# Adds joined in pairs, two down tiles interleaved, six raw weight slots, and another planner for the queues

## The chip, the core and the metric

The kernel runs on one core of a Trainium2 chip. A core has a matrix engine (TensorE, PE, with a queue of its own for loading weights, PEld), a vector engine (VectorE, DVE), a scalar engine (ScalarE, ACT), GpSimd (POOL) and SyncE (SP), which here issues the DMAs. Each works through a queue of its own, and semaphores make one wait for another. TensorE accumulates into banks of PSUM; the other operands lie in SBUF. The metric is the time of one execution on the device, in microseconds. The time before is 2044.98 us, the median of 3 runs (2036.12 to 2045.60).

## What is computed

One layer of a decoder trunk on 2048 tokens of 1024 channels, with 16 learned tokens put ahead and dropped at the end, all in float32:

```
u = rmsnorm(h);  p = u @ w_in                       # 1024 -> 1792
y_a = pool mixer (windows 2, 4, 8, 16)               of p_pool
y_b = conv of 31 taps, layer norm, silu, matrix      of p_bval * sigmoid(p_bgate)
y_c = gelu(p_cgate) * linear scan (conv of 4 taps, two gates)   of p_cx
h = h + concat(y_a, y_b, y_c) @ w_out                # 1024 -> 1024
h = h + square(relu(rmsnorm(h) @ w_up)) @ w_down     # 1024 -> 4096 -> 1024
out = rmsnorm(h)[16:]
```

## The kernel before

**Arithmetic.** A float32 operand is split into a high part (ACT, L108) and a low part (DVE, L109), and a product is three matmuls: high·high, high·low, low·high. A block of weights comes by DMA into a raw slot (tile `wr`, `WR` = 4 of them), and its two parts go into a split slot (tile `wh`, `WH` = 5). `ahead(n)`, called by each item, writes the splits up to `WH` weights ahead of the one in use, and the DMAs `WH` + `WR` ahead. There are 876 such weights.

**Items.** The tokens are worked on in four chunks of 512. A table of items (L864 to L888) gives the order in the program: W, the input projection (14 tiles a chunk); O, the output projection (8 tiles); U, a unit of the up projection; D, a tile of the down projection. W, O and D take 24 matmuls of 512 columns each, 8 blocks of 128 channels times three, with two weights. A chunk has four groups, each of four U and then eight D, which add to the residual `h` (`evac_d`, L801 to L803); the last down group of chunk 3 is done in two halves of 256 columns.

**The up unit.** A unit makes two tiles of 128 channels for 512 tokens. It treats the two halves of the tokens, of the 1024 input channels and of the unit's output channels as 2 × 2 blocks and forms the result from seven products in place of eight (Strassen's scheme in Winograd's form). Each product is 12 matmuls of 256 columns (L285). Its left operands are blocks and sums of blocks of the weights (`gen_sums`, L188 to L200, made once in chunk 0 and kept in DRAM as `sums`), its right operands are seven blocks and sums of blocks of the normed activations (`gen_norm2`, from L701: B11, T2, T3, T1, B21, T4, B22). Seven adds of 256 columns (L782) join the products; then come relu (L793, L795), the square for the high part (L797), the square in float32 (L798) and the low part (L799), which gives the `U` tiles that D reads. The last unit's two tiles are blocks k = 6 and 7 of each D.

**The mixers.** The pool, the convolution of 31 taps (L517, 30 taps of 512 for each of two tiles), its layer norm (from L521, with column sums on PE at L310 and L311 and a reciprocal at L320), the recurrent branch (from L544: its 4-tap convolution, gates, scan) and gelu of the next chunk are written as generators. After each item the program takes some of their work up to a budget. In chunk 0 the weight sums are taken in the same way.

**What sets the order.** The order of the program is only a priority. The tile framework orders each engine's queue by a model of the machine's times; an engine then runs its queue in that order, each instruction when its semaphores allow.

Of the kernel before, what the change touches and what calls it, by code (L numbers as in the profile page):

```python
# [78 lines left out]
def build(nc, tc, x0, xr, w_in, w_out, w_fold, w_up, w_down, vecs, gates, pools, pws, out):  # L79
# [621 lines left out]
    def gen_norm2(o):  # L701
# [57 lines left out]
        yield 1400

    def up_unit(o, u, h0):
# [7 lines left out]

        def product():  # L770
# [3 lines left out]
            ps = ps_main()  # L774
            mm_block(ps[:, :256], wts.hl.pop(h), o.u2[order[h - h0]])
            return ps[:, :256]

        def q_tile():
            return t_("q", 256, 4)

        def add(out, ps, x):
            V.tensor_tensor(out=out, in0=ps, in1=x, op=ALU.add)  # L782

        p1, q, q7, s5 = (q_tile() for _ in range(4))
        A.activation(out=p1, in_=product(), func=AF.Copy)  # L785
        add(q, product(), p1)
        add(q7, product(), q)
        ps = product()
# [265 lines left out]
```

## Time and profile before

| | |
|---|---|
| median of 3 runs | 2044.98 us (2036.12 to 2045.60) |
| the profiled run | 2042.66 us |
| its span | 2040.9 us |
| granted TensorE clock, mean | 0.985 |
| PE busy | 1950.3 us (96%), 11220 matmuls |
| DVE busy | 1587.7 us (78%), 2749 instructions |
| ACT busy | 1119.3 us (55%), 1904 instructions |
| DMA | 297.79 MB, mean 146 GB/s |

A row of the page's groups names line, engine, operation, the tile written and the tiles read (buffer numbers left out), shapes and count; behind the bar stand busy time, mean ns of one, and the idle time just ahead with what ended most of it. A row of the windows gives a stretch, its length, the busy time of PE, PEld, DVE, ACT and POOL with counts, the granted clock, the share of the DMA engines and GB/s. A row of the timeline gives the start, the time up to the end of the run of like instructions, and in brackets idle time ahead with what ended it. The end of a matmul is modelled, so starts say more than ends.

### The profile page before, as it was taken

Reading aid. Unit: us, or ns where it says so; the run is one execution under the profiler, and the core shown is the slowest. Engines: PE = TensorE matmul, PEld = TensorE weight load, DVE = VectorE, ACT = ScalarE, POOL = GpSimd, SP = SyncE. Lnnn points to the kernel's source line nnn. Section 1 sums busy time; section 2 is a strip of 40 time slices with the busy share of each in tenths; the row PEclk is TensorE's granted clock in tenths of the full one; section 3 lists DMA queues with packets and bytes.
Section 4 is the critical chain, followed back from the end, with each engine's and each line's share of the span. In section 5 each row is a group of like instructions: output and inputs, shape, how many; then the busy total and the mean of one; then the engine's idle time right before and its main releaser. Section 6 shows DMA issues by size and latency. Waiting matters only on the chain.

```text
span 2040.9 us, 31716 instructions
## 1 busy us (share of the span) xinstructions
PE 1950.3 (96%) x11220; PEld 1694.6 (83%) x11220; DVE 1587.7 (78%) x2749; ACT 1119.3 (55%) x1904; POOL 0.2 (0%) x4
## 2 busy tenths in 40 slices
PE   8999889899998989999999999999999999999997
PEld 7888688788876779788898778888979878889797
DVE  8987787898988899874776799986768487556477
ACT  6654453635685535664575553664657346345364
POOL 0000000000000000000000000000000000000000
PEclk9999999999998999999999999999999999999999
DMA  6324588737534435353444633444435425544354
GB/s 201 114 78 154 175 255 282 223 114 237 164 106 143 146 98 156 98 156 103 150 119 129 193 102 113 140 117 133 139 108 160 123 79 171 153 131 143 112 167 148
DMA packets 166958, 297.79 MB, mean 146 GB/s; under 512 B 18320, under 2 KB 24592, under 8 KB 166800
## 3 DMA queue, kind: packets, MB, share of 16 engines
q1 hardware_dynamic: 166800, 295.77, 47.7%
q8 instruction: 88, 1.44, 0.3%
q14 instruction: 70, 0.57, 0.1%
HBM read 268.43 MB, written 27.26 MB: 145 GB/s over the span
## 4 chain that ended last, share of the span: by engine, by line
PE 49%; DVE 17%; DMA 15%; ACT 13%; issue 6%; SPq 0%; DVEq 0%; ACTq 0%
PE pm L275 41%; PE pm L285 6%; DMA wr<-sums 6%; DVE wh L109 5%; ACT wh L108 4%; DMA wr<-d_w_down 2%; DMA xr<-d_xr 2%; ACT fr L798 2%; ACT U L797 2%; DVE H L109 1%; ACT fr L795 1%; DVE U L799 1%; DMA s<-d_w_up 1%; DVE fr L782 1%; DVE rs L320 1%
## 5 line engine op out<-in xcount | busy, mean ns | idle before, releaser
L275 PE MATMUL pm<-U,wh 128*128 128x512 f32 (+1 forms) x4272 | 987.7, 390 | 42.4 <-ACT U L797 17.4
L275 PEld LDWEIGHTS pm<-U,wh 128*128 128x128 f32 x4272 | 785.0, 191 | 229.6 <-ACT U L797 24.3
L108 ACT ACTIVATE wh<-wr 128x512 fp32r<-128x512 f32 x876 | 538.2, 627 | 739.5 <-PE pm L275 485.2
L109 DVE TENSOR_TENSOR wh<-wr,wh 128x512 fp32r<-128x512 f32 x876 | 595.3, 686 | 217.1 <-ACT wh L108 213.4
L285 PE MATMUL pm<-H,wh 128*128 128x256 f32 x5376 | 662.6, 284 | 22.0 <-DVE wh L109 9.4
L285 PEld LDWEIGHTS pm<-H,wh 128*128 128x128 f32 x5376 | 650.5, 190 | 35.2 <-DVE wh L109 14.6
L275 PE MATMUL pm<-H,wh 128*128 128x512 f32 (+1 forms) x1344 | 268.0, 357 | 9.3 <-ACT H L373 7.5
L275 PEld LDWEIGHTS pm<-H,wh 128*128 128x128 f32 x1344 | 224.4, 190 | 49.5 <-ACT H L373 7.5
L517 DVE SCALAR_TENSOR_TENSOR ca<-Pbv,vec,ca 128x512 f32<-128x512 f32 x180 | 127.4, 745 | 0.0
L803 DVE TENSOR_TENSOR h<-h,pm 128x512 f32<-128x512 f32 (+1 forms) x106 | 71.3, 673 | 66.7 <-PE pm L275 66.2
L782 DVE TENSOR_TENSOR fr<-pm,q 128x256 f32<-128x256 f32 x256 | 106.5, 417 | 2.3 <-PE pm L285 1.3
L799 DVE TENSOR_TENSOR U<-fr,U 128x512 fp32r<-128x512 f32 x128 | 86.0, 687 | 23.1 <-ACT fr L798 21.7
L782 DVE TENSOR_TENSOR q<-pm,q 128x256 f32<-128x256 f32 x192 | 79.9, 416 | 7.3 <-ACT q L785 3.2
L797 ACT ACTIVATE U<-fr 128x512 fp32r<-128x512 f32 x128 | 77.1, 619 | 0.8
L798 ACT ACTIVATE fr<-fr 128x512 f32<-128x512 f32 x128 | 76.8, 617 | 0.2
L329 DVE TENSOR_TENSOR ss<-ss,fr 128x512 f32<-128x512 f32 (+1 forms) x84 | 53.9, 642 | 13.1 <-ACT fr L328 12.8
L320 DVE RECIPROCAL rs<-rs 128x512 f32<-128x512 f32 (+2 forms) x17 | 53.9, 3168 | 10.9 <-ACT rs L318 10.9
L793 ACT ACTIVATE fr<-fr 128x512 f32<-128x512 f32 x64 | 39.9, 624 | 7.3 <-DVE fr L782 6.7
L517 DVE SCALAR_TENSOR_TENSOR ca<-h,vec,ca 128x512 f32<-128x512 f32 x60 | 42.4, 745 | 0.0
L795 ACT ACTIVATE fr<-fr 128x512 f32<-128x512 f32 x64 | 39.6, 619 | 0.5
L328 ACT ACTIVATE fr<-h 128x512 f32<-128x512 f32 (+1 forms) x45 | 27.4, 617 | 15.8 <-DVE h L697 8.8
L551 DVE SCALAR_TENSOR_TENSOR t<-Pcx,vec,t 128x512 f32<-128x512 f32 x36 | 26.8, 744 | 0.4 <-ACT t L549 0.3
(199 smaller groups left out, 1003.3 us busy)
## 6 DMA issues: line engine op xcount, KB each, us to landing
wr<-d_w_down SPq DMA_DIRECT2D x272, 256.0 KB, 3.0
wr<-sums SPq DMA_DIRECT2D x256, 256.0 KB, 3.3
wr<-d_w_up SPq DMA_DIRECT2D x192, 256.0 KB, 3.2
wr<-d_w_in SPq DMA_DIRECT2D x92, 256.0 KB, 3.2
xr<-d_xr SPq DMA_DIRECT2D x56, 256.0 KB, 3.2
t<-d_w_up SPq DMA_DIRECT2D x32, 256.0 KB, 4.1
wr<-wo_fold SPq DMA_DIRECT2D x32, 256.0 KB, 2.8
wr<-d_w_out SPq DMA_DIRECT2D x32, 256.0 KB, 2.7
```

What stands on the lines that cost most here:

```text
L108: A.activation(out=hi, in_=src, func=AF.Copy)
L109: V.tensor_tensor(out=lo, in0=src, in1=hi.bitcast(F32), op=ALU.subtract)
L275: T.matmul(ps[:, : s1 - s0], w[k // 4][:, a, (k % 4) * P : (k % 4 + 1) * P], rhs[k][:, b, s0:s1], start=(k == 0 and j == 0), stop=(k == KB ...
L285: T.matmul(ps, w[:, a, k * P : (k + 1) * P], op[k // 2][:, b, (k % 2) * 256 : (k % 2) * 256 + 256], start=(k == 0 and j == 0), stop=(k == ...
L320: V.reciprocal(rs[:, c0:c1], rs[:, c0:c1])
L517: V.scalar_tensor_tensor(out=a, in0=o.ub[i][:, k : k + NT], scalar=vc("cw", i * CONVK + k), in1=a, op0=ALU.mult, op1=ALU.add)
L782: V.tensor_tensor(out=out, in0=ps, in1=x, op=ALU.add)
L795: A.activation(out=ra, in_=ra, func=AF.Relu)
L797: A.activation(out=f[:, 0], in_=r, func=AF.Square)
L798: A.activation(out=r, in_=r, func=AF.Square)
L799: V.tensor_tensor(out=f[:, 1], in0=r, in1=f[:, 0].bitcast(F32), op=ALU.subtract)
L803: V.tensor_tensor(out=h, in0=h, in1=ps[:, : s1 - s0], op=ALU.add)
```

## The change

- Raw slots 4 to 6, split slots 5 to 4. PSUM: five banks for products become four, three for the rest become two, and one tile of two banks (`pw`) is new.
- The up unit's products come in another order (B11, B21, T2, T1, T3, B22, T4). Where two products need the same addend or stand side by side, one add of 512 columns joins both (`add2`, with the addend repeated): three of 512 and one of 256. The first result tile is squared after the sixth product; only the second waits for the seventh.
- The operands of an up group are made in another order, with T1, T2, T3 and T4 last.
- `mm_pair`: the first two D tiles of a group do their first six blocks one after the other, 36 matmuls, and then the last two blocks of both.
- Chunk 3's output projection, which stands inside the last down group of chunk 2, begins after two D in place of four.
- The framework's queues are ordered with another model of the machine (`schedule_with_timeline_sim`).

PE does the same matmuls. DVE has 192 instructions fewer; ACT loads its tables 70 times in place of 59.

```diff
-WR = 4
-WH = 5
+WR = 6
+WH = 4
...
-    pm = es.enter_context(tc.tile_pool(name="pm", bufs=5, space=bass.MemoryType.PSUM))
-    pb = es.enter_context(tc.tile_pool(name="pb", bufs=3, space=bass.MemoryType.PSUM))
+    pm = es.enter_context(tc.tile_pool(name="pm", bufs=4, space=bass.MemoryType.PSUM))
+    pw = es.enter_context(tc.tile_pool(name="pw", bufs=1, space=bass.MemoryType.PSUM))
+    pb = es.enter_context(tc.tile_pool(name="pb", bufs=2, space=bass.MemoryType.PSUM))
...
+    def mm_pair(ws, rhs, sub):
+        s0, s1 = sub
+        pss = [ps_main() for _ in ws]
+        for ks in (range(KB - 2), range(KB - 2, KB)):
+            for w, ps in zip(ws, pss):
+                for k in ks:
+                    for j, (a, b) in enumerate(PRODS):
+                        T.matmul(
+                            ps[:, : s1 - s0], w[k // 4][:, a, (k % 4) * P : (k % 4 + 1) * P], rhs[k][:, b, s0:s1],
+                            start=(k == 0 and j == 0), stop=(k == KB - 1 and j == 2),
+                        )
+        return pss
...
+        def add2(out, ps, x):
+            V.tensor_tensor(
+                out=out.rearrange("p (a c) -> p a c", a=2), in0=ps.rearrange("p (a c) -> p a c", a=2),
+                in1=x.unsqueeze(1).broadcast_to([P, 2, 256]), op=ALU.add,
+            )
...
+        px, py, pz = ps_main(), ps_main(), pw.tile([P, 1024], F32, name=nm("pw"), tag="pw")
+        product(px[:, :256])
+        A.activation(out=p1, in_=px[:, :256], func=AF.Copy)
+        product(py[:, :256])
+        product(py[:, 256:])
+        add2(ra, py, p1)
+        q = ra[:, 256:]
+        product(pz[:, 512:768])
+        product(pz[:, 768:])
+        add2(t2, pz[:, 512:], q)
+        px = ps_main()
+        product(px[:, :256])
+        V.tensor_tensor(out=q, in0=px[:, :256], in1=t2[:, :256], op=ALU.add)
+        square(fa, ra)
+        product(pz[:, 256:512])
+        add2(rb, pz[:, 256:768], t2[:, 256:])
+        square(fb, rb)
...
-                items.extend(down[:4])
+                items.extend(down[:2])
                 items.extend(("O", 3, j, full) for j in range(KB))
-                items.extend(down[4:])
+                items.extend(down[2:])
...
+        if kind == "D" and j % KB == 0 and s0 == 0:
+            wts.ahead(wi)
+            ws = [[wts.hl.pop(wi + 2 * i + q) for q in range(2)] for i in range(2)]
+            pss = mm_pair(ws, o.f, (s0, s1))
+            evac_d(o, j // KB, 0, pss[0], s0, s1)
+            held_ps.append(pss[1])
...
-    with tile.TileContext(nc) as tc:
+    with tile.TileContext(nc, schedule_with_timeline_sim=True) as tc:
```

**Three places in the queues.** The rows name line, operation, the tile written and the tiles read (with the number of the buffer) and the shape; xN counts like rows. Lines of the changed kernel stand up to 23 further down: L110 is the split, L532 a tap, L793 `add2`, L818 the add of 256, L802 the low part.

First, DVE in the first up group of chunk 1, about one unit. Before:

```order
L109 TENSOR_TENSOR wh_1420_7837<-wr_1398_7742,wh_1420_7837 128x512
L782 TENSOR_TENSOR fr_1406_7775<-pm_1422_7842,q_1409_7778 128x256
L782 TENSOR_TENSOR q_1410_7779<-pm_1422_7842,q_1408_7777 128x256
L109 TENSOR_TENSOR wh_1423_7857<-wr_1412_7783,wh_1423_7857 128x512
L782 TENSOR_TENSOR fr_1405_7774<-pm_1425_7862,q_1407_7776 128x256
L109 TENSOR_TENSOR wh_1426_7876<-wr_1415_7802,wh_1426_7876 128x512
L782 TENSOR_TENSOR fr_1406_7775<-pm_1428_7881,q_1409_7778 128x256
L517 SCALAR_TENSOR_TENSOR ca_1400_7765<-Pbv_1281_7050,vec_1_66,ca_1400_7765 128x512
L109 TENSOR_TENSOR wh_1429_7896<-wr_1418_7821,wh_1429_7896 128x512
L782 TENSOR_TENSOR fr_1405_7774<-pm_1431_7901,q_1410_7779 128x256
L517 SCALAR_TENSOR_TENSOR ca_1401_7767<-Pbv_1300_7158,vec_1_66,ca_1401_7767 128x512
L109 TENSOR_TENSOR wh_1440_7930<-wr_1421_7840,wh_1440_7930 128x512
```

The same group in the changed kernel:

```order
L110 TENSOR_TENSOR wh_1351_7820<-wr_1330_7699,wh_1351_7820 128x512
L793 TENSOR_TENSOR fr_1340_7778<-pm_1345_7783,q_1343_7781 128x512
L566 SCALAR_TENSOR_TENSOR t_1565_9234<-Pcx_1242_7211,vec_1_69,t_1565_9234 128x512
L110 TENSOR_TENSOR wh_1353_7838<-wr_1332_7716,wh_1353_7838 128x512
L802 TENSOR_TENSOR U_1314_7634<-fr_1316_7636,U_1314_7634 128x512
L532 SCALAR_TENSOR_TENSOR ca_1311_7627<-Pbv_1200_6927,vec_1_69,ca_1311_7627 128x512
L532 SCALAR_TENSOR_TENSOR ca_1312_7629<-Pbv_1218_7031,vec_1_69,ca_1312_7629 128x512
L110 TENSOR_TENSOR wh_1355_7855<-wr_1335_7735,wh_1355_7855 128x512
L802 TENSOR_TENSOR U_1315_7635<-fr_1317_7637,U_1315_7635 128x512
L594 TENSOR_TENSOR t_1420_8317<-t_1420_8317,t_1433_8404 128x512
L110 TENSOR_TENSOR wh_1358_7874<-wr_1337_7757,wh_1358_7874 128x512
L793 TENSOR_TENSOR fr_1342_7780<-pw_1346_7784,fr_1340_7778 128x512
```

Twelve rows held five splits, five adds of 256 and two taps; twelve rows now hold four splits, and all else is 512 wide: adds, taps and work of the recurrent branch (L566, L594) that stood in later groups before. In this whole group, from its first split to that of the next, DVE has 19 taps before and 29 now.

Second, PE at the passage from the second up group of chunk 1 to its down group: the last product (256 columns) and what follows. U_1600 and U_1601 (in the changed kernel U_1486 and U_1487) are the tiles of the third unit; U_1510 is the first tile of the fourth and last. Before:

```order
L285 MATMUL pm_1657_9162<-H_1274_7009,wh_1643_9079 128x256 x6
L275 MATMUL pm_1660_9188<-U_1540_8577,wh_1646_9098 128x512 x3
L275 MATMUL pm_1660_9188<-U_1541_8578,wh_1646_9098 128x512 x3
L275 MATMUL pm_1660_9188<-U_1571_8733,wh_1646_9098 128x512 x3
L275 MATMUL pm_1660_9188<-U_1572_8734,wh_1646_9098 128x512 x3
L275 MATMUL pm_1660_9188<-U_1600_8883,wh_1649_9118 128x512 x3
L275 MATMUL pm_1660_9188<-U_1601_8884,wh_1649_9118 128x512 x3
```

In the changed kernel:

```order
L300 MATMUL pw_1518_8855<-H_1190_6879,wh_1525_8909 128x256 x6
L290 MATMUL pm_1536_8994<-U_1486_8705,wh_1530_8945 128x512
L290 MATMUL pm_1536_8994<-U_1487_8706,wh_1530_8945 128x512 x3
L290 MATMUL pm_1537_8995<-U_1436_8415,wh_1532_8967 128x512
L290 MATMUL pm_1537_8995<-U_1437_8416,wh_1532_8967 128x512 x3
L290 MATMUL pm_1537_8995<-U_1462_8563,wh_1532_8967 128x512 x3
L290 MATMUL pm_1537_8995<-U_1463_8564,wh_1532_8967 128x512 x3
L290 MATMUL pm_1537_8995<-U_1486_8705,wh_1534_8989 128x512 x3
L290 MATMUL pm_1537_8995<-U_1487_8706,wh_1534_8989 128x512 x3
L290 MATMUL pm_1536_8994<-U_1510_8847,wh_1530_8945 128x512
```

Eighteen matmuls of one tile followed the last product; now twenty, and sixteen more of the pair stand ahead of it in the queue.

Third, the layer norm of chunk 0. DVE before, from the low part for the second column sum to the gating with the sigmoid (L540):

```order
L109 TENSOR_TENSOR hl_261_1652<-h_59_262,hl_261_1652 128x512
L320 RECIPROCAL rs_265_1685<-rs_265_1685 128x512
L109 TENSOR_TENSOR wh_267_1699<-wr_246_1521,wh_267_1699 128x512
L537 TENSOR_TENSOR ca_147_754<-ca_147_754,rs_265_1685 128x512
L537 TENSOR_TENSOR ca_148_756<-ca_148_756,rs_265_1685 128x512
L431 TENSOR_TENSOR H_271_1731<-pm_270_1706,rs_58_258 128x512
L540 TENSOR_TENSOR ca_147_754<-ca_147_754,h_59_262 128x512
```

In the changed kernel (L195 to L201 are the weight sums):

```order
L110 TENSOR_TENSOR hl_261_1654<-h_59_264,hl_261_1654 128x512
L200 TENSOR_TENSOR s_301_1887<-s_304_1890,s_301_1887 128x512
L195 TENSOR_TENSOR s_316_1948<-t_315_1947,s_316_1948 128x512
L201 TENSOR_TENSOR t_302_1888<-t_302_1888,s_301_1887 128x512
L335 RECIPROCAL rs_265_1687<-rs_265_1687 128x512
L552 TENSOR_TENSOR ca_147_756<-ca_147_756,rs_265_1687 128x512
L552 TENSOR_TENSOR ca_148_758<-ca_148_758,rs_265_1687 128x512
L196 TENSOR_TENSOR t_315_1947<-s_313_1945,t_315_1947 128x512
L200 TENSOR_TENSOR s_313_1945<-s_316_1948,s_313_1945 128x512
L195 TENSOR_TENSOR s_320_1964<-t_319_1963,s_320_1964 128x512
L201 TENSOR_TENSOR t_314_1946<-t_314_1946,s_313_1945 128x512
L555 TENSOR_TENSOR ca_147_756<-ca_147_756,h_59_264 128x512
```

and PE there (H_286 is the split result of the norm, an operand of the output projection):

```order
L276 MATMUL pm_309_1913<-H_282_1809,wh_289_1830 128x512 x3
L325 MATMUL pb_260_1644<-hl_259_1641,ones_2_71 128x512
L326 MATMUL pb_260_1644<-hl_259_1641,ones_2_71 128x512
L325 MATMUL pb_262_1657<-hl_261_1654,ones_2_71 128x512
L326 MATMUL pb_262_1657<-hl_261_1654,ones_2_71 128x512
L276 MATMUL pm_293_1840<-H_286_1821,wh_275_1769 128x512
```

Before, more than seventy matmuls of 512 columns stood in PE's queue between the second column sum and the first use of the norm's result; now none does, and the weight sums, which came behind the norm on DVE, stand among its rows.

More of the change, by code (lines that the diff above doesn't have):

```diff
@@ L725, in put @@
             split(t[:, 0, :NT], t[:, 1, :NT], raw)
-        b11, b12, t1, b22, t2 = [], [], [], [], []
+        b11, b12, b22, b21, t2 = [], [], [], [], []
         for p in range(2):
@@ L764, in up_unit, with product @@
         o.f += [fa, fb]
-        ra, rb = t_("fr", W0, FR)[:, :NT], t_("fr", W0, FR)[:, :NT]
-        lft, rgt = slice(0, 256), slice(256, 512)
-        order = ("B11", "T2", "T3", "T1", "B21", "T4", "B22")
+        ra, rb, t2 = (t_("fr", W0, FR)[:, :NT] for _ in range(3))
+        p1 = t_("q", 256, 2)
+        order = ("B11", "B21", "T2", "T1", "T3", "B22", "T4")
         nxt = [h0]
-        def product():
+        def product(ps):
             h = nxt[0]
@@ L773, in product, with square @@
             wts.ahead(h)
[L774 to L788, printed above, removed]
-        add(rb[:, rgt], ps, q7)
-        add(s5, ps, q)
-        add(ra[:, lft], product(), p1)
-        add(rb[:, lft], product(), q7)
-        A.activation(out=rb, in_=rb, func=AF.Relu)
-        add(ra[:, rgt], product(), s5)
-        A.activation(out=ra, in_=ra, func=AF.Relu)
-        for f, r in ((fb, rb), (fa, ra)):
+            mm_block(ps, wts.hl.pop(h), o.u2[order[h - h0]])
+        def add2(out, ps, x):
[3 more added lines that the diff above has]
+            )
+        def square(f, r):
+            A.activation(out=r, in_=r, func=AF.Relu)
             A.activation(out=f[:, 0], in_=r, func=AF.Square)
@@ L895, in sources @@
             aps = (
-                (m1, 0), (s, 0), (s, 1024), (s, 1536), (m1, 512), (m2, 512), (s, 512),
+                (m1, 0), (m1, 512), (s, 0), (s, 1536), (s, 1024), (s, 512), (m2, 512),
             )
@@ L924, in build @@
     mixes.append(Mix(ch[0]))
+    held_ps = []
     for n, it in enumerate(items):
@@ L937, in build @@
         wi = windex[n]
+        if kind == "D" and j % KB == 1 and held_ps:
+            evac_d(o, j // KB, j % KB, held_ps.pop(), s0, s1)
+            pump(BUD_D)
+            continue
+        if kind == "D" and j % KB == 0 and s0 == 0:
[4 more added lines that the diff above has]
+            held_ps.append(pss[1])
+            pump(BUD_D)
+            continue
         if kind != "U":
```

36 lines of the change are left out of this document (18 added, 18 removed).

## The prediction

> **What bounds the kernel now.** I read the page first, then the waits, then the busy time by windows, then two stretches of the timeline. The page: the span, the first engine row, TensorE's busy tenths and its granted clock.
>
> ```profile
> span 2040.9 us, 31716 instructions
> ...
> PE 1950.3 (96%) x11220; PEld 1694.6 (83%) x11220; DVE 1587.7 (78%) x2749; ACT 1119.3 (55%) x1904; POOL 0.2 (0%) x4
> ...
> PE   8999889899998989999999999999999999999997
> ...
> PEclk9999999999998999999999999999999999999999
> ```
>
> TensorE (PE) is busy 96%, so 2040.9 − 1950.3 = 90.6 us are left to win, plus what half-clock stretches cost. PE sets the end; the question is where it is made to wait, and for whom. The waits (engine and line, whom for, us in total, times, longest):
>
> ```profile
> ACT wh L108 <- DMA wr<-sums: 88.0, 71, 3.9
> ...
> PE pm L275 <- ACT U L797: 17.4, 15, 2.3
> ...
> PE pm L275 <- DVE U L799: 12.1, 14, 1.4
> ...
> PE pm L285 <- DVE wh L109: 9.4, 20, 1.4
> ```
>
> PE's largest waits (17.4 + 12.1 us) are for the squares of an up group's last unit. The 88.0 us that ScalarE (ACT) waits for raw weights is no PE time by itself: ACT is idle 45%. The windows (stretch, length, then busy us of PE, PEld, DVE, ACT and POOL with counts, then granted clock):
>
> ```profile
> 348.00:397.00 49.00, 43.98 (x342) 41.30 (x341) 42.24 (x87) 26.93 (x50) 0.00 (x0) 1.00 0.82 254
> 397.00:444.00 47.00, 45.45 (x197) 36.32 (x196) 46.34 (x76) 18.77 (x31) 0.00 (x0) 1.00 0.37 108
> 444.00:486.00 42.00, 42.00 (x346) 41.53 (x345) 38.76 (x74) 26.86 (x50) 0.00 (x0) 1.00 0.67 201
> 581.00:637.00 56.00, 47.97 (x189) 35.71 (x188) 48.93 (x77) 47.41 (x73) 0.00 (x0) 0.94 0.20 59
> 687.00:775.00 88.00, 82.88 (x348) 66.41 (x347) 84.43 (x148) 34.37 (x56) 0.00 (x0) 0.96 0.34 101
> 774.00:815.00 41.00, 41.00 (x343) 40.77 (x342) 38.70 (x74) 27.02 (x50) 0.00 (x0) 1.00 0.56 167
> 1262.00:1304.00 42.00, 41.77 (x345) 41.24 (x344) 39.02 (x75) 26.98 (x50) 0.00 (x0) 1.00 0.54 160
> 1303.00:1313.00 10.00, 7.42 (x32) 5.57 (x32) 8.91 (x17) 6.39 (x11) 0.00 (x0) 1.00 0.51 150
> 1666.00:1718.00 52.00, 46.93 (x342) 44.03 (x341) 43.49 (x85) 33.75 (x63) 0.00 (x0) 0.93 0.47 140
> ```
>
> These are, in order: up group 1, down group 1 and up group 2 of chunk 0; its last down group; the input projection of chunk 2; the first up groups of chunks 1 and 2; one passage from up to down; the first up group of chunk 3. Two things are to be seen. VectorE (DVE) is nearly full in the middle of the program: 84.43 of 88, 38.70 of 41. And an up group of 41 us leaves it some 3 us. Whoever puts more DVE work into an up group makes PE wait, since every weight passes through DVE (the split at L109) before PE may read it.
>
> **Prices.** Four rows of the page's groups (busy us, then mean ns of one), and one stretch of the timeline (start, duration, engine, line, operation, count, and in brackets the idle time ahead):
>
> ```profile
> L275 PE MATMUL pm<-U,wh 128*128 128x512 f32 (+1 forms) x4272 | 987.7, 390 | 42.4 <-ACT U L797 17.4
> ...
> L109 DVE TENSOR_TENSOR wh<-wr,wh 128x512 fp32r<-128x512 f32 x876 | 595.3, 686 | 217.1 <-ACT wh L108 213.4
> L285 PE MATMUL pm<-H,wh 128*128 128x256 f32 x5376 | 662.6, 284 | 22.0 <-DVE wh L109 9.4
> ...
> L517 DVE SCALAR_TENSOR_TENSOR ca<-Pbv,vec,ca 128x512 f32<-128x512 f32 x180 | 127.4, 745 | 0.0
> ```
>
> ```profile
> 1297.80 2.41 PE L285 MATMUL pm<-H,wh 128*128 128x256 f32 x19
> ...
> 1299.71 1.29 DVE L109 TENSOR_TENSOR wh<-wr,wh 128x512 fp32r<-128x512 f32 x2
> ...
> 1301.85 0.41 DVE L782 TENSOR_TENSOR fr<-pm,q 128x256 f32<-128x256 f32 x1
> 1302.18 0.41 DVE L782 TENSOR_TENSOR q<-pm,q 128x256 f32<-128x256 f32 x1
> ...
> 1303.18 4.35 PE L275 MATMUL pm<-U,wh 128*128 128x512 f32 x18
> ...
> 1305.96 0.42 DVE L782 TENSOR_TENSOR fr<-pm,q 128x256 f32<-128x256 f32 x1
> ...
> 1306.99 0.61 ACT L797 ACTIVATE U<-fr 128x512 fp32r<-128x512 f32 x1
> 1307.73 1.41 DVE L517 SCALAR_TENSOR_TENSOR ca<-Pbv,vec,ca 128x512 f32<-128x512 f32 x2
> ...
> 1309.05 1.50 DVE L799 TENSOR_TENSOR U<-fr,U 128x512 fp32r<-128x512 f32 x2
> ...
> 1309.22 0.49 PE L275 MATMUL pm<-U,wh 128*128 128x512 f32 x1 [1.68 <-ACT U L797]
> ...
> 1310.61 1.67 PE L275 MATMUL pm<-U,wh 128*128 128x512 f32 x6 [0.90 <-DVE U L799]
> ```
>
> Durations overlap, so I price by the step from one start to the next. A pair of two-operand DVE operations of 512 takes 1.29 us where one takes 0.686, so the step is 0.60; a tap (three-operand, 512) steps 1.41 − 0.745 = 0.66; an add of 256 steps 1302.18 − 1301.85 = 0.33. PE: (2.41 − 0.284)/18 gives 0.118 for a matmul of 256 columns, (4.35 − 0.39)/17 gives 0.233 for 512. A product of 12 matmuls is 1.42 us, an up group of 28 products 39.6, a down group of 8 × 24 matmuls 44.7.
>
> **The change, part by part.**
>
> 1. Fewer adds. A unit did seven adds of 256 (7 × 0.33 = 2.3 us) and now does three of 512 and one of 256 (3 × 0.60 + 0.33 = 2.1). The 192 instructions saved are worth some 0.2 us a unit on DVE: nothing.
>
> 2. From up to down. In the stretch above, PE does 18 matmuls of the first down tile (ending 1307.5) and waits, because the last chain add (1305.96), the squares and the subtraction (1309.05) are later. The window 1303 to 1313 loses 10.00 − 7.42 = 2.6 us. Now the chain of one half starts a product earlier, and PE has 36 matmuls of two tiles (8.4 us) that need neither; in the order shown, 20 of them (4.7 us) stand behind the last product and 16 ahead of it. The chain that is left (add 0.69, three steps of ACT and a subtraction at 0.6 to 0.7, some 5 us with the waits seen) is then hidden, so the wait goes; if the cover failed, all 2.6 us would be back. Of 16 passages, 12 lie outside the stretches of part 4, where nothing is won: −31 us (bounds: 12/16 of 29.5, −22, and 16 × 2.6, −41).
>
> 3. Operands of chunk 3. Chunk 3's output projection moves two down items earlier, so six items of 24 × 0.233 = 5.6 us stand behind it, which cover the making of the up operands, in place of four: 33 us, not 22. The window 1666 to 1718 loses 5.1 us idle and 7% of its clock, 3.6 us. I take −8 (bounds 0 and −8.7).
>
> 4. The order of the engines' work. Counting in DVE's queue from the split of a group's first weight to the split of the next group's first, with the steps above:
>  - up 1, down 1, up 2 of chunk 0: 45.1 + 37.0 + 46.3 = 128.4 us before, 62.6 + 44.0 + 66.1 = 172.7 now; the added rows are 16 taps, 9 first taps of the recurrent branch's convolution, gates, and parts of the making of weight sums. PE's matmuls in that stretch: 39.6 + 43.6 + 43.3 = 126.5.
>  - first up group of chunk 1: 44.7 before; now 57 two-operand and 50 three-operand rows of 512, 3 adds of 256 and 2.3 us of others, 57 × 0.60 + 50 × 0.66 + 1.0 + 2.3 = 70.6. PE 43.6.
>  - first up group of chunk 2: 45.3 before, 68.6 now. PE 43.3.
>
>  DVE runs its queue in order, and the first down weight stands behind all of it. What protects PE is the lead: four slots of split weights, of which three can still be unread when the first up weight is split, 3 × 12 × 0.233 = 8.4 us. Five slots gave 11.2. So PE loses at least DVE's sum less its own less the lead. I add 2% for idle DVE time (bounds 0, and 4% as in the window at 687, where DVE paced and was busy 84.43 of 88): 172.7 × 1.02 − 8.4 − 126.5 = 41.3, less the 5.0 + 1.6 + 0 that the three windows lose now: +35; chunk 1: 72.0 − 8.4 − 43.6 = +20; chunk 2: 70.0 − 8.4 − 43.3 = 18.3, less 0.2: +18. In all +73 (bounds +36, if half of it hides, and +79 with 4%).
>  The same work is gone elsewhere: the last down group of chunk 0 falls from 49.8 to 19.6 us of DVE, the projection of chunk 2 from 82.6 to 75.5, that of chunk 3 from 78.7 to 75.5. The windows 581 to 637 (8.0 us lost) and 687 to 775 (5.1, and 4% of the clock, 3.5) give back at most 16.6; I take −15 (bounds −17 and −6).
>  The Trainium skill, "Perfetto Trace Analysis", section "Tensor Engine Instruction (MATMUL, LD_WEIGHTS)", states that ScalarE and VectorE are strict first-in first-out, and that only TensorE's queue can pull weight loads ahead. By that rule the +73 stands; if VectorE could pass a tap to reach a split, it would be 0 and the sum 73 us less.
>
> 5. The layer norm of chunk 0. Rows of the timeline, before:
>
> ```profile
> 154.13 0.40 PE L311 MATMUL pb<-hl,ones 128*128 128x512 f32 x1
> ...
> 160.51 0.40 PE L311 MATMUL pb<-hl,ones 128*128 128x512 f32 x1
> ...
> 160.75 5.48 PE L275 MATMUL pm<-H,wh 128*128 128x512 f32 x23
> ...
> 163.12 3.35 DVE L320 RECIPROCAL rs<-rs 128x512 f32<-128x512 f32 x1 [2.82 <-ACT rs L318]
> ...
> 166.07 11.31 PE L275 MATMUL pm<-U,wh 128*128 128x512 f32 x48
> ...
> 171.14 1.29 DVE L540 TENSOR_TENSOR ca<-ca,h 128x512 f32<-128x512 f32 x2 [2.33 <-ACT h L539]
> ```
>
>  Between the second column sum (160.51) and the norm's result (172.4, and 0.6 for a split) stand 71 matmuls in PE's queue. In the new order none stands there, nor between the first sum (154.53) and the second. The chain's own 6.4 + 12.1 = 18.5 us becomes PE idle time, less what of it was other DVE work, more the weight sums that now stand in it: +17 (bounds +12.1, the second leg alone, and +25, with one more such leg of 6.4).
>
> 6. Six raw slots take ACT's 88.0 us of waiting for raw weights away. ACT's idle 45% hides it: 0 (bounds 0 and −9.4, PE's wait for L109). Tables are loaded 70 times in place of 59, on ACT, off the path: 0.
>
> Sum: −31 − 8 + 73 − 15 + 17 = +36. The profiled run took 2042.66 us, 2.3 below the median shown: 2042.7 + 36 = **2078**.
>
> **A word on the clock.** The window 1666 to 1718 shows 0.93 with 5.1 us of idle time. Inside a stretch paced by DVE a lower clock is hidden: 43.6/0.93 = 46.9, still below 72. Only down group 1 (43.6 against 44.0) would feel it, +3. The Trainium skill, "TensorE: Matmul & The Clock Gate", section "What's actually happening", says that the array falls to half clock after an idle window of about 3.4 us and needs as long a busy one to recover; by it, only the 17 us stall of part 5 would add some 2 us, an estimate from that page.
>
> **Rivals.**
>
> - *Faster, about 2018.* The new machine model takes nearly all the other losses away too. PE idles 90.6 us, and lower clocks cost up to 1.5% of the span, 31 us more; of these 122, take out the 6.8 counted in part 4: 2042.7 + 73 + 17 − 115 = 2018. It is no longer slower from where 90 of the 115 go; I count 54. For it: the small waits (20 times for L109) are spread everywhere. Against: the start, the end and the first input projections stay as they are.
> - *About the same, 2045.* The DVE surplus is half hidden (+36) and the layer norm costs 12: 2042.7 + 36 + 12 − 31 − 8 − 7 = 2045. For it: 38.70 us busy in 41 is below the 44.7 that I priced for that group, since part of it runs ahead in the lead. Against: a queue in order can't run ahead further than its slots.
> - *Much slower, about 2108.* In the crowded up groups DVE is not only full but blocked: a tap or a gate that waits for ACT, or an add for PE, holds the splits behind it. Its place is the same three stretches, 312 us of DVE; at 10% idle in place of 2 that is +25, and with only 26 of the 31 us won at the passages, 2078 + 30. It decides once DVE's idle time there passes 5%. For it: ACT has 53 us in the group of chunk 1 too, and the window 581 to 637 has both DVE (48.93) and ACT (47.41) short of its 56 us, so each waited for the other.
> - *The passages don't close.* The down weights of the pair come late, since DVE is behind: 2042.7 + 73 + 17 − 8 − 15 = 2110. This goes with the case before.
>
> **How the numbers follow.** Forecast 0.50, its own range 2058 to 2098; much slower (both) 0.20; about the same 0.13; faster 0.17. The predicted time is 2078. The range takes in the cases to both sides until about one in ten is left out at either end: 2022 to 2112. A measurement of this kernel tells about 0.5%, 10 us. Slower by more: 0.70; within: 0.13; faster by more: 0.17.
>
> **What would show it.** The window over the first up group of chunk 1 should last 60 to 66 us in place of 40, with DVE busy over 90% and PE under 75%; waits of PE's up products for the split (L110 now) should grow from 9.4 us to 40 or more; the waits for U should nearly vanish; PE should stand still some 17 us ahead of the first output projection. If that group still takes 42 us, part 4 is wrong, and with it the sign.

## The result and the profile after

The changed kernel takes 2114.65 us (median of 4 runs, 2109.82 to 2116.88) against 2045.29 us for the kernel before on the same chip: 1.0338 times as long, 95% interval 1.0291 to 1.0385. It is slower, as forecast, but by 69 us where 36 were forecast, and the time lies just outside the range that ended at 2112.

The page of the changed kernel: PE does the same 11220 matmuls, and its share falls from 96% to 93%.

```profile
span 2115.1 us, 31261 instructions
...
PE 1971.1 (93%) x11220; PEld 1724.4 (82%) x11220; DVE 1589.8 (75%) x2557; ACT 1149.0 (54%) x1915; POOL 0.2 (0%) x4
```

DVE has 192 instructions fewer and is busy as long as before (1589.8 against 1587.7 us): adds of 512 in place of pairs of 256 saved nothing. PE's waits after (columns as before):

```profile
PE pm L300 <- ACT wh L109: 37.4, 24, 3.3
PE pm L276 <- ACT H L109: 12.3, 1, 12.3
PE pw L300 <- DVE fr L793: 12.1, 11, 2.9
PE pb L325 <- ACT hl L109: 11.9, 4, 9.0
PE pm L300 <- DVE wh L110: 11.3, 8, 2.6
```

The waits for the squares (17.4 and 12.1 us before) are gone from the head of the list. In their place PE waits in the up products (L300) for split weights, 37.4 + 11.3 = 48.7 us in these two rows, and for the layer norm of chunk 0 (12.3 us at the output projection, 9.0 us as the longest wait at its column sums). The windows after, in the order up 1, down 1, up 2 of chunk 0 (a chunk's groups count from 0, so these are its second up group, the down group behind it and its third up group), first and second up group of chunk 1, first of chunks 2 and 3, then the first output projection, the last down group of chunk 0 and the projection of chunk 2:

```profile
377.00:431.00 54.00, 44.35 (x332) 41.55 (x331) 53.62 (x96) 33.25 (x58) 0.00 (x0) 0.97 0.61 190
431.00:489.00 58.00, 49.93 (x200) 38.66 (x200) 52.00 (x84) 22.78 (x35) 0.00 (x0) 0.91 0.58 178
489.00:553.00 64.00, 53.90 (x345) 51.13 (x343) 61.73 (x102) 50.35 (x82) 0.00 (x0) 0.84 0.37 110
815.00:882.00 67.00, 52.75 (x352) 48.58 (x350) 66.52 (x110) 55.21 (x88) 0.00 (x0) 0.90 0.37 107
932.00:981.00 49.00, 43.10 (x325) 41.85 (x324) 41.00 (x63) 39.51 (x68) 0.00 (x0) 0.93 0.47 139
1327.00:1390.00 63.00, 50.83 (x347) 46.91 (x345) 62.59 (x101) 53.21 (x86) 0.00 (x0) 0.92 0.38 109
1745.00:1802.00 57.00, 49.05 (x348) 46.38 (x347) 53.00 (x82) 36.23 (x66) 0.00 (x0) 0.94 0.56 172
178.00:250.00 72.00, 48.18 (x195) 37.33 (x195) 45.14 (x66) 29.94 (x46) 0.00 (x0) 0.81 0.61 193
642.00:689.00 47.00, 47.00 (x211) 38.35 (x211) 26.50 (x43) 20.63 (x36) 0.00 (x0) 1.00 0.36 108
736.00:815.00 79.00, 77.68 (x334) 62.51 (x333) 74.59 (x129) 37.42 (x59) 0.00 (x0) 1.00 0.34 104
```

The first up group of chunk 1 took 41 us with PE full; now 67, of which DVE is busy 66.52. That is what a queue that sets the pace looks like: DVE at 99%, PE with idle time and a clock of 0.90. PE's last wait there is mostly for ACT's half of a split (6.8 us, against 1.2 us for DVE's), but ACT in its turn waited 10.1 us for PE to free slots, while DVE was idle for 0.5 us. Two of the signs that the prediction named did not come so: PE was busy 79% of that window, not under 75%, and of the longer waits for split weights most are for ACT's half (L109), not for DVE's (L110). The last down group of chunk 0 (642 to 689) has been relieved: DVE is busy 26.50 of 47 us.

### The profile page after: what moved, and what is told of

It reads as the page before. It is cut to its first block, busy times and chain, and to the rows that moved or that the text cites. A ratio compares the mean times of both kernels' runs of the same rounds, so it can differ in the third digit from the quotient of the medians.

```text
span 2115.1 us, 31261 instructions
## 1 busy us (share of the span) xinstructions
PE 1971.1 (93%) x11220; PEld 1724.4 (82%) x11220; DVE 1589.8 (75%) x2557; ACT 1149.0 (54%) x1915; POOL 0.2 (0%) x4
## 4 chain that ended last, share of the span: by engine, by line
PE 64%; DVE 8%; ACT 5%; issue 3%; DMA 1%; DVEq 0%; ACTq 0%; SPq 0%
PE pm L276 35%; PE pm L300 12%; PE pw L300 9%; PE pm L290 7%; DVE wh L110 2%; DVE ca L532 1%; ACT wh L109 1%; DVE fr L793 1%; ACT L582 1%; DVE h L837 0%; ACT t L577 0%; DVE U L802 0%; DMA xr<-d_xr 0%; ACT L587 0%; DMA s<-d_w_up 0%
## 5 line engine op out<-in xcount | busy, mean ns | idle before, releaser
L109 ACT ACTIVATE wh<-wr 128x512 fp32r<-128x512 f32 x876 | 546.3, 628 | 767.8 <-PE pm L276 441.7
L110 DVE TENSOR_TENSOR wh<-wr,wh 128x512 fp32r<-128x512 f32 x876 | 596.7, 686 | 225.5 <-ACT wh L109 219.6
L300 PE MATMUL pm<-H,wh 128*128 128x256 f32 x3072 | 411.3, 286 | 55.4 <-ACT wh L109 37.4
L300 PEld LDWEIGHTS pm<-H,wh 128*128 128x128 f32 x3072 | 390.2, 192 | 68.8 <-ACT wh L109 43.1
L300 PE MATMUL pw<-H,wh 128*128 128x256 f32 x2304 | 327.6, 298 | 18.8 <-DVE fr L793 12.1
L300 PEld LDWEIGHTS pw<-H,wh 128*128 128x128 f32 x2304 | 311.7, 205 | 25.8 <-DVE fr L793 15.8
L276 PE MATMUL pm<-H,wh 128*128 128x512 f32 (+1 forms) x1344 | 274.7, 362 | 20.0 <-ACT H L109 12.3
L276 PEld LDWEIGHTS pm<-H,wh 128*128 128x128 f32 x1344 | 228.6, 193 | 61.9 <-ACT H L109 12.8
L826 DVE TENSOR_TENSOR h<-h,pm 128x512 f32<-128x512 f32 (+1 forms) x106 | 70.3, 674 | 111.2 <-PE pm L276 66.3
L532 DVE SCALAR_TENSOR_TENSOR ca<-Pbv,vec,ca 128x512 f32<-128x512 f32 x180 | 132.0, 741 | 1.8 <-ACT ca L529 1.6
L802 DVE TENSOR_TENSOR U<-fr,U 128x512 fp32r<-128x512 f32 x128 | 87.4, 683 | 18.2 <-ACT fr L801 18.2
L793 DVE TENSOR_TENSOR fr<-pw,fr 128x512 f32<-128x512 f32 x128 | 87.8, 686 | 9.9 <-PE pw L300 7.7
L344 DVE TENSOR_TENSOR ss<-ss,fr 128x512 f32<-128x512 f32 (+1 forms) x84 | 53.6, 642 | 2.6 <-ACT fr L343 2.3
L793 DVE TENSOR_TENSOR fr<-pm,q 128x512 f32<-128x512 f32 x64 | 44.0, 687 | 1.4 <-PE pm L300 0.3
```

Source lines behind the costliest of these rows:

```text
L109: A.activation(out=hi, in_=src, func=AF.Copy)
L110: V.tensor_tensor(out=lo, in0=src, in1=hi.bitcast(F32), op=ALU.subtract)
L276: T.matmul(ps[:, : s1 - s0], w[k // 4][:, a, (k % 4) * P : (k % 4 + 1) * P], rhs[k][:, b, s0:s1], start=(k == 0 and j == 0), stop=(k == KB ...
L300: T.matmul(ps, w[:, a, k * P : (k + 1) * P], op[k // 2][:, b, (k % 2) * 256 : (k % 2) * 256 + 256], start=(k == 0 and j == 0), stop=(k == ...
L532: V.scalar_tensor_tensor(out=a, in0=o.ub[i][:, k : k + NT], scalar=vc("cw", i * CONVK + k), in1=a, op0=ALU.mult, op1=ALU.add)
L793: V.tensor_tensor(out=out.rearrange("p (a c) -> p a c", a=2), in0=ps.rearrange("p (a c) -> p a c", a=2), in1=x.unsqueeze(1).broadcast_to([ ...
```

## The experiments

Two rival causes stood at the start. **A:** the new machine model puts DVE's work where the up groups can't bear it. **B:** the code itself costs (a tile of two banks for which each unit waits, fewer banks, four split slots). Below, "old model" and "new model" are the two ways of ordering the queues; "4+5" means 4 raw and 5 split slots.

**The model alone, taken from the change.**

```diff
-    with tile.TileContext(nc, schedule_with_timeline_sim=True) as tc:
+    with tile.TileContext(nc, schedule_with_timeline_sim=False) as tc:
```

> The changed kernel with the old machine model ordering the queues, all else as changed. Theory A (the new model's order crowds DVE in up groups): counted in DVE's queue as in the prediction, up 1 + down 1 + up 2 of chunk 0 fall from 172.7 to 127.4 us, the first up groups of chunks 1 and 2 from 70.7 and 68.6 to 44.0 and 43.3; so those stretches lose at most 5 us each, the stall at the first layer norm goes, while the last down group of chunk 0 and the projections of chunks 2 and 3 go back to pacing by DVE (+24). Expected 2115 - 121 + 24, about 2018 us, 2000 to 2035. Rival B (the code itself costs: one tile of two banks that each unit waits for, fewer banks, four split slots): the time stays above 2080.

Measured: 2009.02 us, 0.985 of before (0.9825 to 0.9874). Cause A: with the new code as it is, taking the new order away takes all the loss away, and more. In the windows of this kernel the first and second up groups of chunk 1 are back at 40 and 41 us, with PE full:

```profile
775.00:815.00 40.00, 39.91 (x334) 39.60 (x334) 39.80 (x67) 27.68 (x52) 0.00 (x0) 1.00 0.56 171
863.00:904.00 41.00, 40.15 (x330) 39.35 (x330) 34.86 (x59) 34.26 (x61) 0.00 (x0) 1.00 0.53 164
```

**The model alone, added to the kernel before.**

```diff
-    with tile.TileContext(nc) as tc:
+    with tile.TileContext(nc, schedule_with_timeline_sim=True) as tc:
```

> The kernel before with the new machine model ordering the queues, nothing else. Theory A: DVE's sums are 63.6 + 40.4 + 68.5 = 172.5 us for up 1, down 1, up 2 of chunk 0, 68.6 and 69.7 for the first up groups of chunks 1 and 2, so +75 there, -20 where DVE is relieved, and the passages from up to down stay open: 2095 to 2130 us. Rival B: the order alone is harmless, 2035 to 2055 us.

Measured: 2083.3 us, 1.021 (1.0182 to 1.0237). The model costs the old code 2.1%, less than expected: the first up groups of chunks 1 and 2 lasted 62.2 and 64.3 us, near what their sums say, but the passages closed too, which I hadn't expected of the order alone. PE's wait for the squares fell from 17.4 + 12.1 us to 0.4.

**The slots under the new model.** The changed kernel with the old numbers:

```diff
-WR = 6
-WH = 4
+WR = 4
+WH = 5
```

> The changed kernel with the old numbers of slots, 4 raw and 5 split. Theory A: the lead of PE's weights is one weight longer, 2.8 us in each of three paced stretches, and the sums that the planner gives are 163.7, 65.0 and 65.5 in place of 172.7, 70.7 and 68.6: -9 -6 -3 -8, so about 2090 us (2080 to 2105). Rival: the slots decide nothing, within 10 us of 2115; or the raw slots are what helped, above 2125.

Measured: 2081.51 us, 1.0203 (1.0181 to 1.0226). Against the change's 1.0338 that is 1.35% of 2040, some 28 us, where 25 were expected. Whether the fewer raw or the more split slots did it, a run with 5+5 tells:

> The changed kernel with 5 raw and 5 split slots. Theory E (under the new model the fifth split slot is worth what 4+5 gained over 6+4, since PE's lead over the splits is longer and the planner's sums smaller: 162.9, 63.8 and 64.2 us in place of 172.7, 70.7 and 68.6): 2065 to 2085 us. Rival: the fewer raw slots were what helped there, for whatever reason; then above 2095.

Measured: 2079.44 us, 1.0198 (1.0179 to 1.0217), the same as 4+5. So it is the fifth split slot, as far as these three kernels tell (6+5 was not run). The slots also move the planner's order: the first up group of chunk 1 falls by 14.0 us (66.3 to 52.3), and 6.9 of these are in DVE's sum (70.7 to 63.8, table below). The windows of this kernel for the first and second up group of chunk 1:

```profile
805.00:857.00 52.00, 42.46 (x300) 40.09 (x298) 51.66 (x86) 44.20 (x72) 0.00 (x0) 0.90 0.37 112
911.00:951.00 40.00, 37.44 (x302) 36.49 (x300) 33.85 (x51) 31.56 (x54) 0.00 (x0) 1.00 0.52 159
```

The second group lasts 40 us where it took 49 with four, though with 302 matmuls in it in place of 325. And the kernel before, new model, with 6+4:

> The kernel before with the new model and 6 raw and 4 split slots, which completes the table of code, model and slots. Theory E: DVE's sums are 63.7 + 42.3 + 66.7 = 172.7, 72.8 and 71.6, all a little above the same code with 4 and 5 (172.5, 68.6, 69.7), and the lead is 2.8 us shorter in each crowded stretch: 2095 to 2115 us. Rival: the raw slots gain 30 us here as they did under the old model, 2050 to 2065.

Measured: 2105.28 us, 1.0323 (1.0304 to 1.0343), against 2083.3 with 4+5: the short lead costs the old code as well, and that kernel is nearly as slow as the whole change. New model and four split slots are nearly all of the loss.

**The down tiles without the pair** (changed code, old model, 6+4):

```diff
-        if kind == "D" and j % KB == 0 and s0 == 0:
+        if False and kind == "D" and j % KB == 0 and s0 == 0:
```

> As the first kernel of this group (changed code, old model), but each down tile done alone, without the interleaving of the first two. Theory: the pair closes the passages, 16 x 1.8 to 2.6 us, so this is 25 to 40 us slower than the first. Rival: the earlier squaring of one half closes them by itself; then within 10 us of the first.

Measured: 2003.07 us, 0.9821 (0.9798 to 0.9844), 6 us below the kernel with the pair where 25 to 40 above had been expected: a miss (the rival, that the earlier squaring closes them by itself, allowed 10 us). It is not the interleaving that closes the passages: without it PE's wait for the squares is not among its larger waits either.

**The slots alone, in the kernel before** (old model):

```diff
-WR = 4
-WH = 5
+WR = 6
+WH = 4
```

> The kernel before with 6 raw and 4 split slots, old model. Theory C (raw weights that come late are part of the open passage: ACT waited 2.07 + 1.00 us for down weights there, ahead of the squares): the passages close in part, -10 to -25, so 2015 to 2032 us. Rival D (the chain of add, relu, squares and subtraction alone holds the passage): within 8 us of 2040, or slower by the shorter lead.

Measured: 2004.5 us, 0.9847 (0.9827 to 0.9867), lower than either expectation. Two constants give as much as the whole code under the old model. ACT's wait for down weights before, and in this kernel that wait and PE's for the low parts:

```profile
ACT wh L108 <- DMA wr<-d_w_down: 39.3, 35, 4.1
...
ACT wh L108 <- DMA wr<-d_w_down: 5.1, 4, 2.2
...
PE pm L275 <- DVE U L799: 1.2, 2, 0.7
```

Before, ACT waited 39.3 us for raw down weights and PE 17.4 + 12.1 us for the squares; nearly all of both is gone together. The passage from up to down in chunk 2, two rows of the timeline before, then a stretch of this kernel's:

```profile
1303.09 1.28 ACT L108 ACTIVATE wh<-wr 128x512 fp32r<-128x512 f32 x2 [2.07 <-DMA wr<-d_w_down]
...
1306.45 0.63 ACT L108 ACTIVATE wh<-wr 128x512 fp32r<-128x512 f32 x1 [1.00 <-DMA wr<-d_w_down]
```

```profile
1288.57 0.62 ACT L793 ACTIVATE fr<-fr 128x512 f32<-128x512 f32 x1
...
1289.13 4.28 PEld L275 LDWEIGHTS pm<-U,wh 128*128 128x128 f32 x19
...
1289.22 0.63 ACT L797 ACTIVATE U<-fr 128x512 fp32r<-128x512 f32 x1
1289.25 8.08 PE L275 MATMUL pm<-U,wh 128*128 128x512 f32 x34
...
1292.23 1.28 DVE L799 TENSOR_TENSOR U<-fr,U 128x512 fp32r<-128x512 f32 x2
...
1293.57 3.56 PEld L275 LDWEIGHTS pm<-U,wh 128*128 128x128 f32 x16 [0.16 <-DVE U L799]
```

The down group begins at 1289.25, and the low parts start 2.98 us later; before, they started 5.87 us after the down group's first matmul (1309.05 − 1303.18). What had been late in the chain was a weight: in the kernel before, ACT stood at splits whose raw weights hadn't landed (2.07 and 1.00 us), with the relu and the squares behind them in its queue. PE's order is the same at this passage: 19 matmuls stand ahead of the first use of one of these low parts in both kernels (18 and 1 before, in the prediction's rows; here the 20th weight load is the one that waits for the low part, 0.16 us). On ACT one split that stood ahead of the first square (1306.45) now stands behind it. The 2.89 us gained are about the 3.07 us of waits that went, which speaks for the landing of the weights; a kernel with more raw slots and the old order on ACT was not run, so this isn't shown.

**The new unit without the new slots** (changed code, old model, no pair, 4+5; the slots are edited as above):

> The changed code with the old model, the down tiles one by one and the old slots 4 and 5: that leaves the joined adds, the earlier squaring, the new operand order, the new banks and the earlier output projection of chunk 3. If the earlier squaring closes the passages by itself: 2000 to 2012 us. If the raw slots of theory C are what closes them: 2020 to 2035 us.

Measured: 2020.7 us, 0.9925 (0.9905 to 0.9944), at the lower edge of the second expectation, that of the raw slots. PE's wait for the low parts falls to 2.9 us here, so the passages are mostly closed by this code too (the earlier squaring is the likely part of it; nothing here runs it alone), though ACT still waits 31.0 us for down weights; what it gains is half of what the slots gain.

**Five of both** (changed code, old model, no pair):

```diff
-WR = 6
-WH = 4
+WR = 5
+WH = 5
```

> As the kernel with 4 raw and 5 split slots, with 5 of both. Both theories let it be no slower than either of the kernels with 4 and 5 or 6 and 4: 1992 to 2006 us. It is the candidate for a version that beats both.

Measured: 1995.87 us, 0.98 (0.9781 to 0.9819): better than the kernel before and than the change, and within what was expected.

**DVE's load, taken away.** The changed kernel with a third of the taps:

```diff
-        for k in range(1, CONVK):
+        for k in range(1, 11):
```

> The changed kernel (new model) with 10 of the 30 taps of the long convolution, so that its output isn't the reference's: 40 DVE operations of 0.66 us a chunk are left out. Theory A (DVE's queue paces the crowded up groups): the planner's new order gives 157.0 us of DVE in place of 172.7 for up 1, down 1, up 2 of chunk 0, 55.0 and 55.3 in place of 70.7 and 68.6 for the first up groups of chunks 1 and 2, and 32.6 in place of 40.2 for the second ones, so the first up group of chunk 1 lasts about 51 us in place of 66 and the whole 2050 to 2065 us, 50 to 60 less. Rival (ACT, with 53 us there, or the single two-bank tile sets the pace): that group stays above 60 us and the whole above 2090.

Measured: 2052.92 us, 1.0079 (1.0055 to 1.0103). The first up groups of chunks 1 and 2 took 51.6 and 52.0 us; 51 had been expected. Windows of the one in chunk 1 and of up 2 of chunk 0:

```profile
795.00:846.00 51.00, 45.90 (x348) 43.70 (x346) 47.97 (x81) 45.85 (x78) 0.00 (x0) 0.97 0.44 135
...
472.00:535.00 63.00, 50.06 (x354) 46.63 (x353) 51.98 (x88) 55.72 (x89) 0.00 (x0) 0.94 0.38 117
```

The forecast for chunk 0 failed. Its up 1, down 1 and up 2 were to need 157.0 us of DVE in place of 172.7, and lasted 53.6 + 55.1 + 62.6 = 171.3 us, where they had lasted 175.6. In up 2 DVE's sum is some 50 us, and the group lasts 62.6; ACT is the busier engine (55.72 of 63 us), and PE's 12.4 us of waits for weights are all for ACT's half. So with DVE's load gone ACT holds that group at nearly the old length, as the rival had it for chunk 1. The new order crowds both queues there: in up 2 ACT was busy 26.86 us before and 50.35 us in the change. That the whole still fell as forecast is in part luck, since the first up group of chunk 0 began at 255.3 us in place of 267.4, which the expectation did not count.

In the first up group of chunk 1 ACT's work fell as well (55.21 to 45.85 us busy), since the planner moved other rows, so this run alone doesn't part DVE from ACT there. The lengths over all runs do, for the first up groups (and up 1 of chunk 0 in one run):

| kernel | split slots | group | DVE's sum, us | length, us | length less sum |
|---|---|---|---|---|---|
| the change | 4 | first up, chunks 1 and 2 | 70.7, 68.6 | 66.3, 63.1 | −4.4, −5.5 |
| old code, new model, 6+4 | 4 | the same | 72.8, 71.6 | 69.2, 70.2 | −3.6, −1.4 |
| 10 taps | 4 | the same | 55.0, 55.3 | 51.6, 52.0 | −3.4, −3.3 |
| no weight sums (below) | 4 | up 1, chunk 0 | 73.8 | 71.8 | −2.0 |
| old code, new model, 4+5 | 5 | first up, chunks 1 and 2 | 68.6, 69.7 | 62.2, 64.3 | −6.4, −5.4 |
| the change, 4+5 | 5 | the same | 65.0, 65.5 | 54.5, 54.2 | −10.5, −11.3 |
| the change, 5+5 | 5 | the same | 63.8, 64.2 | 52.3, 53.0 | −11.5, −11.2 |

(The sum is DVE's queue between the first splits of this group and the next, with the steps of the prediction; the length runs from the first matmul with one of those weights to the first with the other.) In these groups the length is the sum less a lead of 1 to 6 us with four slots and 5 to 12 with five; up 2 of chunk 0 with 10 taps, above, is not one of them. ACT's sums, some 43 to 55 us, stay below every length. Two kernels part the engines best: the old code with 4+5 and the 10 taps have nearly the same sum on ACT in the first up group of chunk 1 (some 47 and 46 us), but 68.6 and 55.0 us on DVE, and the group lasts 62.2 and 51.6.

**The layer norm of chunk 0.** The changed kernel without the weight sums' arithmetic:

```diff
-        V.tensor_tensor(out=a22, in0=a21, in1=a22, op=ALU.add)
-        V.tensor_tensor(out=a21, in0=a11, in1=a21, op=ALU.subtract)
...
-        V.tensor_tensor(out=a11, in0=a22, in1=a11, op=ALU.subtract)
-        V.tensor_tensor(out=a12, in0=a12, in1=a11, op=ALU.subtract)
```

> The changed kernel with the four DVE operations of the weight sums left out (the loads and stores stay, so the output isn't the reference's). PE's queue around the first layer norm is the same. Theory F (the norm's own chain makes PE stand still, 18.5 us as in the prediction): the 72 us from the first output projection to the next input projection, which lose 27, still lose 16 to 21. Rival G (the weight sums among the norm's rows make it): they lose under 10. The whole falls in both cases, by 20 to 40 us, since the first up group of chunk 0 also has less DVE work.

Measured: 2104.96 us, 1.0325 (1.0303 to 1.0347). The stretch at the norm lost 22.4 us (27.2 with the sums): a little more than F said, and far from G. The norm's own chain makes the wait; the sums add some 5 us. The whole did not fall by 20 to 40, a miss: without the sums the planner put 73.8 us of DVE into up group 1 of chunk 0, which then took 71.8 us in place of 54.0.

**More mixer work in the down groups** (as the kernel with five of both):

```diff
-BUD_D = 3000
+BUD_D = 5000
```

> The changed code, old model, down tiles one by one, 5 raw and 5 split slots, with a larger budget for mixer work after each down tile (5000 in place of 3000). DVE's sum in the last down group of chunk 0 falls from 49.1 to 33.2 us, in the others it rises by 1 to 9 and stays below PE's 44. Expected 6 to 14 us below the same kernel with 3000 (1996): 1982 to 1990. Rival: DVE's work in the whole of chunk 0 sets the end there wherever it lies, within 4 us of 1996.

Measured: 1992.44 us, 0.9774 (0.9755 to 0.9793). Its interval overlaps that of the kernel with 3000 (0.9781 to 0.9819), so whether the budget helps stays open; the 6 to 14 us that were expected are not reached. It is the lowest time of all.

The table of code, model and slots, as ratios to before:

| code | model | 4+5 | 6+4 | 5+5 |
|---|---|---|---|---|
| before | old | 1 | 0.9847 | |
| changed, no pair | old | 0.9925 | 0.9821 | 0.9800 |
| changed | old | | 0.9850 | |
| before | new | 1.0210 | 1.0323 | |
| changed | new | 1.0203 | 1.0338 | 1.0198 |

## Why the prediction was wrong in size

The direction, the mechanism and the three stretches were right. One class of stretches was put at nothing that cost 22.6 us, and several terms were mis-sized, most of them the same way. PE's loss in a stage is its length less the steps of its matmuls; after less before:

| step of the prediction | forecast | measured |
|---|---|---|
| 4: the three crowded stretches | +73 | +38.1 + 22.5 + 19.1 = +79.7 |
| 4: relief elsewhere | −15 | −23.7 |
| 5: layer norm of chunk 0 (the first output projection, and the stretch behind it) | +17 | +26.3 − 5.6 = +20.7 |
| 2: passages (12 down groups) | −31 | −30.8 |
| 3: operands of chunk 3 | −8 | +1.9 |
| up groups counted as free (second of chunks 1 and 2, first of chunk 0) | 0 | +7.4 + 6.7 + 8.5 = +22.6 |
| the start and the rest | 0 | +4.3 |
| sum | +36 | +74.7 |

The spans of the two profiled runs differ by 2115.1 − 2040.9 = 74.2; the medians differ by 69.

**Step 4 was right in its mechanism, and its lead too long.** The first up group of chunk 1 was to last 60 to 66 us; it lasts 66.3. The sum took off a lead of 8.4 us in each stretch. The table of lengths gives 4.4 and 5.5 us for chunks 1 and 2, and the stretch of chunk 0 lasts 175.6 us, which is more than its sum of 172.7. The Trainium skill, "Perfetto Trace Analysis", section "Tensor Engine Instruction (MATMUL, LD_WEIGHTS)", has VectorE and ScalarE strict first-in first-out; the table of lengths agrees with it, to within a lead of 1 to 12 us.

**The step that failed is the list of stretches to which step 4 was applied.** It names three, and puts every other up group at nothing without giving a reason; three of these cost 22.6 us more than before. I took an up group as free where DVE's sum was about PE's. The second up group of chunk 1 has 40.2 us of DVE and 39.4 of PE, so by the sum nothing is lost, and 9.5 us are. A sum over a whole group assumes a lead as long as the group's unevenness. With four split slots the lead in an up group is three products, 3 × 1.42 = 4.3 us, and the queues in it are uneven by more. The timeline of the changed kernel there:

```profile
957.79 1.28 ACT L577 ACT_TABLE_LOAD   x1
...
960.37 1.28 ACT L582 ACT_TABLE_LOAD   x1
...
963.95 0.61 ACT L109 ACTIVATE wh<-wr 128x512 fp32r<-128x512 f32 x1
...
964.62 0.50 PE L300 MATMUL pm<-H,wh 128*128 128x256 f32 x2 [1.84 <-ACT wh L109]
...
967.56 1.28 ACT L587 ACT_TABLE_LOAD   x1
...
969.50 1.28 ACT L554 ACT_TABLE_LOAD   x1
...
971.85 0.61 ACT L109 ACTIVATE wh<-wr 128x512 fp32r<-128x512 f32 x1
...
972.52 0.51 PE L300 MATMUL pw<-H,wh 128*128 128x256 f32 x2 [1.15 <-ACT wh L109]
```

ACT, whose tables I had put off the path at 0 (step 6), does not split one weight from 957.79 to 963.95 (6.2 us) nor from 967.56 to 971.85 (4.3 us): it loads tables and works on the gates and the sigmoid, with a relu and a square of an up unit between. PE runs dry, and DVE itself waits 5.0 us in this group for ACT's half of a split. PE's waits in the group, 5.9 us, are all for ACT's half too, so here it was ACT and not DVE that held the weights back. With five split slots this group loses 1.9 (4+5) or 3.6 us (5+5) in place of 9.5. The planner's order differs too in those kernels, so the shorter lead and the new order are not parted there.

The first up group of chunk 0 (+8.5) is another case. DVE's sum there is some 53 us before and after, well above PE's, and what has grown is waiting for DMA:

```profile
305.85 0.63 ACT L109 ACTIVATE wh<-wr 128x512 fp32r<-128x512 f32 x1 [3.38 <-DMA wr<-sums]
...
306.43 0.69 DVE L196 TENSOR_TENSOR t<-s,t 128x512 f32<-128x512 f32 x1 [4.92 <-DMA s<-d_w_up]
...
307.85 0.51 PE L300 MATMUL pm<-H,wh 128*128 128x256 f32 x2 [3.32 <-ACT wh L109]
```

DVE stood 4.92 us at a weight sum whose block hadn't landed, ACT 3.38 us at a split of the sums, and PE behind them 3.32 us. No run takes this wait alone away, so its share of the 8.5 us stays open.

**Step 6 was wrong in its reason.** Six raw slots were costed at 0, since ACT is idle 45%. In the kernel before, the new pair of slot numbers is worth 32 us: ACT's idle share is no cover for a wait that stands ahead of the squares in ACT's queue. Step 2 had the size of the passages (−30.8 against −31), but by luck: it credited the unit and the pair. The slots alone, the new unit's code for the most part, and the new model's order alone each close them, so their gains don't add, and the pair adds none that can be seen.

**Step 3.** In the old model the change does what the step says: the first up group of chunk 3 loses 4.9 us in place of 11.3. Under the new one it loses 13.2, and the old code 19.9. The order took back what the move gave.

**Step 5** had the mechanism, and its sum came near partly by luck: the stage itself loses 26.3 us more than before, above the bound of 25, and 5.6 us that the step didn't count are won back behind it. Rows of the timeline after:

```profile
181.13 0.50 PE L325 MATMUL pb<-hl,ones 128*128 128x512 f32 x1 [0.59 <-ACT hl L109]
...
182.56 0.69 PE L326 MATMUL pb<-hl,ones 128*128 128x512 f32 x1 [0.93 <-DVE hl L110]
...
192.26 0.80 PE L325 MATMUL pb<-hl,ones 128*128 128x512 f32 x1 [9.01 <-ACT hl L109]
...
194.00 0.80 PE L326 MATMUL pb<-hl,ones 128*128 128x512 f32 x1 [0.95 <-DVE hl L110]
...
198.13 3.35 DVE L335 RECIPROCAL rs<-rs 128x512 f32<-128x512 f32 x1
...
207.14 5.05 PE L276 MATMUL pm<-H,wh 128*128 128x512 f32 x15 [12.34 <-ACT H L109]
```

PE idles 9.01 and 12.34 us, then steps by (5.05 − 0.39)/14 = 0.33 us a matmul where 0.233 is its pace. The granted clock (third figure from the end) says why:

```profile
183.00:207.00 24.00, 1.84 (x3) 0.58 (x2) 19.75 (x28) 9.33 (x13) 0.00 (x0) 0.50 0.81 259
207.00:210.00 3.00, 2.86 (x7) 2.24 (x8) 2.91 (x6) 1.21 (x3) 0.00 (x0) 0.50 0.67 253
210.00:213.00 3.00, 3.00 (x15) 2.42 (x14) 1.68 (x3) 0.63 (x1) 0.00 (x0) 1.00 0.51 184
```

It is half while PE stands still, and full again from 210, 2.9 us after PE's restart at 207.14. The stage lost 27.2 us, of which 0.59 + 0.93 + 9.01 + 0.95 + 12.34 = 23.8 is idle time; the other 3.4 us are put down to matmuls at half clock, some of them the column sums between the idle times. The Trainium skill, "TensorE: Matmul & The Clock Gate", section "What's actually happening", has half the clock until a busy window of about 3.4 us has passed; the trace agrees roughly, with 2.9 us.

**The clock in the crowded stretches** was hidden, as said: 0.84 in up 2 of chunk 0, which still took 64.1 us against a DVE sum of 66.1.

**The rivals.** The much slower one (2108) came closest in time but not in mechanism: DVE wasn't blocked in the three stretches (idle for 9.5 of the 306 us of their windows, 3%, where that case needed 5%); other groups lost. In one of those, the first up group of chunk 0, DVE was indeed blocked, but by a DMA.

## What to carry to other kernels

When a planner reorders a program, count each in-order engine's work between the first weights of successive stages, but compare it with the other engines in pieces as long as the lead that the slots give, not by the stage. A wait of an engine that is mostly idle is on the path as soon as something urgent stands behind it in its queue. And time the parts apart: here two constants gained 1.5%, the planner's model lost 2 to 5%, and the time of the whole change showed neither.

## What had not been expected

The same pair of constants, 6 raw and 4 split slots, gained 1.5% under one order (0.9847) and lost 1.1 to 1.4% under the other (1.0323 against 1.0210; 1.0338 against 1.0198 and 1.0203). Under the old order the raw slots' wait was on the path and the split slots' lead wasn't; under the new one it was the reverse. A table of two models and two numbers of slots was needed to see it; each of the edits alone would have been judged by the order that it happened to meet.
